# Banded attention: weights times values in float32r passes, with the high and low parts of the values as one stationary operand

## The chip, the cores and the metric

The kernel runs on one core of one Trainium2 chip. The metric is the device time of one execution in microseconds (us), over several executions; lower is better. One execution was also recorded by the profiler, and every row below comes from that one.

## What is computed

Two blocks follow each other on 512 tokens of 1024 features, all in float32. The first block (an mLSTM and stick-breaking attention, then an MLP) is not touched. The second block has two hybrid layers, and each holds a sliding-window attention of 16 heads of 64 features, with two heads for keys and values:

```
s = jnp.einsum('bnqkgd,bnskd->bnkgqs', qb, kw) * ATT_SCALE     # blocks of 128 queries, 256 keys
s = jnp.where(mask, s, NEG_INF)                                # the band: the last 128 keys
p = jax.nn.softmax(jnp.concatenate([s, sink], axis=-1), axis=-1)[..., :-1]
o = jnp.einsum('bnkgqs,bnskd->bnqkgd', p, vw)                  # weights times values: the change is here
...
o_a = o * jax.nn.silu(z_a)
y = jnp.einsum('bse,ed->bsd', jnp.concatenate([o_h, o_a], axis=-1), w_out)
return x + rms_norm_2(y, g_post)
```

The other half of a hybrid layer is a recurrence (`hgrn2`) of 8 heads, whose result `o_h` goes through the first half of `w_out`.

## The kernel before

The large products split each float32 operand into a high and a low part in float32r, a format that TensorE takes in one pass, and add three products (`mm3`, lines 142 to 150: high by high, low by high, high by low). A group is one output tile of 128 by 512, made of 24 such matmuls. `load_w` (lines 127 to 140) brings weights by DMA (queue SP) into three raw buffers `wr`; ScalarE (ACT) makes the high part `wh`, VectorE (DVE) the low part `wl`. Smaller products run as plain float32 matmuls; the profile shows each of those as two records.

**The attention** is `swa_pair(p)`, for two heads each, called eight times a layer. Per head h, in this order:

- scores: 8 float32r matmuls into two banks of PSUM (`xa`, line 531), with stationary operand of 128 columns;
- mask and minimum: four VectorE instructions (line 537) into two pages `prp` of the buffer ring `ha` (4 buffers); four exponentials on ScalarE (line 539), then one small one for the sink (line 543);
- the sum, its reciprocal and four scalings on VectorE (lines 544, 545, 548);
- 7 transposes on TensorE into two banks `xb` (lines 553, 555), copied to `pT` in ring `hb` by ScalarE (lines 557, 559);
- weights times values: 7 float32 matmuls (lines 563, 565) with 64 stationary columns into one bank `po` of tag `xc`. The two heads of a pair share that bank, on 64 partitions each, and one VectorE instruction (line 567) multiplies it by the gate page `zt` and stores `oa[p]`.

**What sets the order.** The code is written in program order with priorities; a scheduler then puts the instructions of each engine into a fixed order, and each engine runs its own list in order. Buffers of one tag are handed out in the order of the code: a tile waits until the one whose buffer it takes is free. In PSUM, tag `xc` has one buffer, and tag `mt` (`K.pmt()`) has one. `mt` is used by the query projection (`proj_qa`, transposes of line 465), and by the loop at line 601 that transposes the eight recurrence heads into `T1`.

The code of a layer runs, as far as it matters here: the last two projections `proj_qa(1)` and `proj_za(1)` (8 groups), pairs 0 to 3 of the attention with a priority above them, the eight transposes into `T1` (line 601, ScalarE line 604, VectorE line 605), pairs 4 to 7, then the output projection `wo1` (8 groups, which need `T1` alone) and `wo2` (8 groups, which need all of `oa`). The results of `wo1` are copied out by ScalarE (line 617); those of the last two blocks of tokens go into pages of tag `on`, which `oa[4]` to `oa[7]` use too.

Of the kernel before, what the change touches and what calls it, by code (L numbers as in the profile page):

```python
# [17 lines left out]
P = 128  # L18
# [40 lines left out]
class Kern:  # L59
# [42 lines left out]
    def above(self, mark):  # L102
        """Priority above everything emitted since mark."""
        return self.tc.high_priority(self.tc.cur_priority - mark + 4000)
# [4 lines left out]
    def rsqrt(self, ms, tag=None, bufs=4):  # L109
        """1/sqrt of a small positive tile."""  # L110
        p, n = ms.shape[0], ms.shape[1]
        y = self.small(n, tag or f"rsy{n}", bufs, p)
        e = self.nhalf[:p, 0:1] if n == 1 else self.nhalf[:p, 0:1].to_broadcast([p, n])
        self.nc.gpsimd.tensor_tensor(y, ms, e, ALU.pow)  # L114
        return y

    def later(self, f):
        """Emit f after the evacuation of the next product."""
        self.new.append(f)
# [5 lines left out]

# [1 line left out]
    def load_w(self, src, n=S, prio=20000):  # L127
# [14 lines left out]
    def mm3(self, ps, st, mv):  # L142
        """ps += sum_k st[k].T @ mv[k], each operand a (hi, lo) pair."""
        nc = self.nc
        n = len(st)
        for k in range(n):
            (sh, sl), (mh, ml) = st[k], mv[k]
            nc.tensor.matmul(ps, sh, mh, start=(k == 0), stop=False)  # L148
            nc.tensor.matmul(ps, sh, ml, start=False, stop=False)  # L149
            nc.tensor.matmul(ps, sl, mh, start=False, stop=(k == n - 1))  # L150
# [24 lines left out]

# [1 line left out]
    def new_T(self):  # L177
# [12 lines left out]
    def bcast2(self, page, src):  # L190
        """A row of 1024 on every partition, as two pages."""
        out = []
        for i in range(2):
            t = page()
            self.nc.sync.dma_start(out=t, in_=src[i * S:(i + 1) * S].partition_broadcast(P))
            out.append(t)
        return out

    def prep(self, gsrc, page, wk, T):
        """Returns f(tb, pages): rms norm of a token block (two [128, 512] pages), transposed and split into T."""  # L200
        nc = self.nc
        g = self.bcast2(page, gsrc)

        def do(tb, x):
            xn = [wk(), wk()]
            ss = [self.small(1, f"ss{i}", 4) for i in range(2)]
            for i in range(2):
                nc.scalar.activation(xn[i], x[i], AF.Square, scale=D ** -0.5, accum_out=ss[i])
            rs = self.rms(ss)
            c = slice(tb * P, (tb + 1) * P)  # L210
            for i in range(2):
                nc.vector.scalar_tensor_tensor(xn[i], x[i], rs, g[i], ALU.mult, ALU.mult)
                ps = self.psum("xa" if i else "xb").rearrange("p (k t) -> p k t", k=4)
                for k in range(4):
                    nc.tensor.transpose(ps[:, k, :], xn[i][:, k * P:(k + 1) * P], self.ident)
                self.split(T[0][i][:, :, c], T[1][i][:, :, c], ps)
        return do

    def rms(self, ss):
        """1/sqrt(ss[0] + ss[1] + eps)."""  # L220
        s = self.small(1, "rmss", 4)
        self.nc.gpsimd.tensor_scalar(s, ss[0], ss[1], EPS, ALU.add, ALU.add)
        return self.rsqrt(s)
# [24 lines left out]
def layer(K, l, xd, win, wout, gpost, lbp, ghead, sinks, out, gnext):  # L248
    """One hybrid layer: K.hT and xd (DRAM rows of x) -> out (DRAM), and the next layer's K.hT."""
    nc, tc = K.nc, K.tc  # L250
    if True:
# [9 lines left out]
        def hb():  # L261
            return page("hb", 4)

        # lower bounds: [128, 8] tiles, feature f = 128 h + p
        lb = K.lc.tile([P, 2, 8], F32, name=f"lb{l}")
# [178 lines left out]
        def rope(dst, ps, tb, nh):  # L444
            """dst, ps: [128, nh * 64]."""
            a = ev()[:, :nh * 64]
# [31 lines left out]
        def proj_kv():  # L478
            quad = K.quad(F32R)
            kT.extend((quad[:, i, :], quad[:, 2 + i, :]) for i in range(2))  # L480
            va.append(page("va", 1).rearrange("p (c d) -> p c d", c=NT))

# [11 lines left out]
            def evac(tb, ps):  # L494
                nc.scalar.copy(va[0][:, tb, :], ps[:, P:2 * P])
                r = ev()
                rope(r[:, 0:P], ps[:, 0:P], tb, 2)
                K.later(lambda: turn(tb, r))
# [13 lines left out]
        def swa_pair(p):  # L512
            kv = p // 4
            zt = page("zs", 2)
            nc.sync.dma_start(out=zt, in_=za_d[p * P:(p + 1) * P, :])
            po = K.psum("xc", 1)
            for e in range(2):
                h = 2 * p + e
                r = slice(64 * e, 64 * e + 64)
                pT = [hb().rearrange("p (s t) -> p s t", s=2) for _ in range(2)]  # L520
                pn, den = K.small(NT, "pn", 4), K.small(NT, "den", 4)
# [27 lines left out]
                for i in range(2):  # L549
                    pt = K.psum("xb").rearrange("p (s t) -> p s t", s=2)  # L550
                    for s in range(2):
                        sb = 2 * i + s
                        nc.tensor.transpose(pt[:, s, 0:P], Ps[sb][0][:, P:2 * P], K.ident)  # L553
                        if sb + 1 < NT:
                            nc.tensor.transpose(pt[:, s, P:2 * P], Ps[sb + 1][0][:, 0:P], K.ident)
                    if i == 0:
                        nc.scalar.copy(pT[i], pt)
                    else:
                        nc.scalar.copy(pT[i].rearrange("p s t -> p (s t)")[:, :384], pt.rearrange("p s t -> p (s t)")[:, :384])
                vv = slice(64 * kv, 64 * kv + 64)  # L560
                for n in range(NT):
                    o = po[r, n * P:(n + 1) * P]
                    nc.tensor.matmul(o, va[0][:, n, vv], pT[n // 2][:, n % 2, 0:P], start=True, stop=(n == 0))  # L563
                    if n:
                        nc.tensor.matmul(o, va[0][:, n - 1, vv], pT[(n - 1) // 2][:, (n - 1) % 2, P:2 * P],  # L565
                                         start=False, stop=True)
            nc.vector.tensor_tensor(oa[p], po, zt, ALU.mult)

# [26 lines left out]

        # head outputs, transposed, head norm gain applied in the split
        T1 = K.new_T()
# [58 lines left out]
def block1(K, xd, prm, win, wout, wup, wdown, bif, gmix, gmlp, out, gnext):  # L656
# [13 lines left out]
    with ExitStack() as octx:  # L670
# [40 lines left out]

# [1 line left out]
        v1 = {}  # L713
# [28 lines left out]

        # gates: rows 0-7 input, rows 32-39 forget; rows 64-103 the products of the low parts of the weights
        raw = ma()[:, :P].rearrange("p (k n) -> p k n", k=KT)
# [173 lines left out]

# [1 line left out]
        qb, ks, kb, vb, rq = {}, {}, {}, {}, {}  # L920

        def proj_qkb(c, is_q):
            """Head norms, then 4 heads transposed: [128 d, 4 heads, 512 t]."""
            quad = bq.tile([P, 4, S], F32, name=K.nm("qk"), tag="q" if is_q else "k", bufs=2)
# [112 lines left out]

# [1 line left out]
    K.stp = K.ctx.enter_context(tc.tile_pool(name="st", bufs=1, reuse_waits="tile"))  # L1039
# [106 lines left out]
```

## Time and profile before

| | |
|---|---|
| median of 3 executions | 1870.59 us (1868.47 to 1870.9) |
| span of the profiled execution | 1868.7 us |
| TensorE (PE) busy | 1828.8 us, 98% |
| VectorE (DVE) busy | 1033.3 us, 55% |
| ScalarE (ACT) busy | 828.5 us, 44% |
| attention heads of layer 1 and of layer 2 | some 1133 to 1305 and 1625 to 1797 us |

The page gives no separate time for the profiled execution; its span lies at the lower end of the timed ones, so that what lies around the span is under about 2 us. PE rows are matmuls and PEld rows the loads of their stationary operand. A matmul's duration is longer than the distance to the next one, since matmuls are pipelined: for a cost, the distance between starts is read. [...]

### The profile page before, as it was taken

The numbers are of one execution on the slowest core, as the hardware profiler recorded it, in microseconds if no ns is written. First come the engines' busy times: TensorE is split into PE (matmuls) and PEld (weight loads), VectorE is DVE, ScalarE is ACT, GpSimd is POOL, SyncE is SP. The second block draws the span as 40 slices with busy tenths as digits, with TensorE's granted clock in tenths as the row PEclk, the third lists the DMA queues.
The fourth block names the chain that finished last, engine by engine and source line by source line (L and its number), as shares of the span: only waits on it lengthen the run. The fifth ranks groups of instructions, "written<-read, shape, count | busy, mean of one in ns | idle before, by whom it ended". The sixth has DMA issues, their size and how long they took to land.

```text
span 1868.7 us, 29367 instructions
## 1 busy us (share of the span) xinstructions
PE 1828.8 (98%) x11696; PEld 1498.3 (80%) x11696; DVE 1033.3 (55%) x2162; ACT 828.5 (44%) x1687; POOL 136.1 (7%) x191
## 2 busy tenths in 40 slices
PE   7999999999999999999999999999999999999998
PEld 5777788787798888888888888878878888888786
DVE  4364545546554444446474666756265648575733
ACT  4456634344342323233443445656344345374641
POOL 1001111010000000000000001100130001101002
PEclk9999999999999999999999999999999999999999
DMA  6252433231432222334323232322343222422222
GB/s 185 60 105 63 102 75 85 67 90 45 147 101 92 90 90 90 106 108 141 111 80 103 69 105 95 108 91 71 105 163 97 92 74 93 127 88 74 74 91 101
DMA packets 103442, 180.09 MB, mean 96 GB/s; under 512 B 8960, under 2 KB 19584, under 8 KB 103304
## 3 DMA queue, kind: packets, MB, share of 16 engines
q1 hardware_dynamic: 103304, 178.20, 31.9%
q8 instruction: 92, 1.51, 0.3%
q14 instruction: 46, 0.38, 0.1%
HBM read 163.48 MB, written 14.70 MB: 95 GB/s over the span
## 4 chain that ended last, share of the span: by engine, by line
PE 89%; DMA 4%; ACT 3%; DVE 2%; issue 1%; POOL 0%; SPq 0%; ACTq 0%; DVEq 0%
PE mm L148 24%; PE mm L150 24%; PE mm L149 24%; DMA wr<-in_w_in_dram 2%; PE xc L563 2%; PE xa L531 1%; PE xc L565 1%; PE xc L993 1%; PE xa L975 1%; PE xb L553 1%; DMA pg<-xs 1%; PE xc L427 1%; ACT wh L136 1%; PE xc L419 1%; PE xa L372 1%
## 5 line engine op out<-in xcount | busy, mean ns | idle before, releaser
L136 ACT CAST wh<-wr 128x1024 fp32r<-128x1024 f32 (+1 forms) x272 | 282.1, 1039 | 327.2 <-PE mm L150 146.6
L137 DVE TENSOR_TENSOR wl<-wr,wh 128x1024 fp32r<-128x1024 f32 (+1 forms) x272 | 328.7, 1214 | 168.6 <-ACT wh L136 80.7
L148 PE MATMUL mm<-wh,hh 128*128 128x512 f32 (+1 forms) x896 | 348.8, 390 | 10.3 <-ACT hh L604 4.4
L149 PE MATMUL mm<-wl,hh 128*128 128x512 f32 (+1 forms) x896 | 348.0, 389 | 0.0
L150 PE MATMUL mm<-wh,hl 128*128 128x512 f32 (+1 forms) x896 | 347.1, 391 | 0.0
L148 PE MATMUL mm<-hh,wh 128*128 128x512 f32 x640 | 255.3, 399 | 6.8 <-ACT pg L730 6.2
L150 PE MATMUL mm<-hh,wl 128*128 128x512 f32 x640 | 253.8, 397 | 0.8 <-DVE wl L137 0.8
L149 PE MATMUL mm<-hl,wh 128*128 128x512 f32 x640 | 253.2, 396 | 0.0
L148 PEld LDWEIGHTS mm<-wh,hh 128*128 128x128 f32 x896 | 169.3, 189 | 45.4 <-ACT hh L604 5.2
L149 PEld LDWEIGHTS mm<-wl,hh 128*128 128x128 f32 x896 | 169.0, 189 | 32.8 <-DVE wl L137 1.1
L150 PEld LDWEIGHTS mm<-wh,hl 128*128 128x128 f32 x896 | 168.1, 189 | 31.6 <-DVE hl L188 0.3
L148 PEld LDWEIGHTS mm<-hh,wh 128*128 128x128 f32 x640 | 121.0, 189 | 34.2 <-ACT pg L730 8.0
L150 PEld LDWEIGHTS mm<-hh,wl 128*128 128x128 f32 x640 | 120.9, 189 | 27.7 <-DVE wl L137 2.0
L149 PEld LDWEIGHTS mm<-hl,wh 128*128 128x128 f32 x640 | 121.0, 189 | 24.8 <-issue 0.2
L148 PE MATMUL mm<-qd,wh 128*128 128x512 f32 (+1 forms) x288 | 105.3, 366 | 0.0
L149 PE MATMUL mm<-qd,wh 128*128 128x512 f32 (+1 forms) x288 | 105.3, 366 | 0.0
L150 PE MATMUL mm<-qd,wl 128*128 128x512 f32 (+1 forms) x288 | 105.1, 366 | 0.0
L148 PE MATMUL mm<-wh,ah 128*128 128x512 f32 x256 | 100.3, 392 | 0.2 <-ACT wk L1075 0.2
L149 PE MATMUL mm<-wl,ah 128*128 128x512 f32 x256 | 99.6, 389 | 0.0
L150 PE MATMUL mm<-wh,al 128*128 128x512 f32 x256 | 99.6, 389 | 0.0
L114 POOL TENSOR_TENSOR sm<-sm,nhalf 128x4 f32<-128x4 f32 (+1 forms) x64 | 59.9, 936 | 505.4 <-DVE sm L436 329.6
L1085 DVE TENSOR_TENSOR qd<-mm,qd 128x512 f32<-128x512 f32 x64 | 44.1, 688 | 58.5 <-PE mm L150 58.4
(294 smaller groups left out, 2768.7 us busy)
## 6 DMA issues: line engine op xcount, KB each, us to landing
wr<-in_w_in_dram SPq DMA_DIRECT2D x160, 512.0 KB, 4.7
wr<-in_w_out_dram SPq DMA_DIRECT2D x40, 512.0 KB, 4.3
wr<-in_w_up_dram SPq DMA_DIRECT2D x32, 512.0 KB, 4.3
wr<-in_w_down_dram SPq DMA_DIRECT2D x32, 512.0 KB, 4.5
zh<-pg SPq DMA_DIRECT2D x16, 256.0 KB, 2.1
pg<-zh SPq DMA_DIRECT2D x16, 256.0 KB, 2.9
za<-pg SPq DMA_DIRECT2D x16, 256.0 KB, 2.0
pg<-za SPq DMA_DIRECT2D x16, 256.0 KB, 2.6
```

What stands on the lines that cost most here:

```text
L114: self.nc.gpsimd.tensor_tensor(y, ms, e, ALU.pow)
L136: nc.scalar.copy(hi, raw)
L137: nc.vector.tensor_tensor(lo, raw, hi.bitcast(F32), ALU.subtract)
L148: nc.tensor.matmul(ps, sh, mh, start=(k == 0), stop=False)
L149: nc.tensor.matmul(ps, sh, ml, start=False, stop=False)
L150: nc.tensor.matmul(ps, sl, mh, start=False, stop=(k == n - 1))
L372: nc.tensor.matmul(pl[32 * j:32 * j + 32, o0 + 32 * c:o0 + 32 * c + 32], k[:, o:o + 32], q[:, o:o + 32])
L419: nc.tensor.matmul(pS[:, c, :], kt[:, c, :], v[c][:, vc])
L427: nc.tensor.matmul(po[:, c, :], ST[:, c, :], v[c][:, vc], start=True, stop=(c == 0))
L531: nc.tensor.matmul(psc[:, i, 2 * P - wi:], qT[p][e][:, t1 - P:t1], kT[kv][j][:, t1 - wi:t1], start=(j == 0), stop=(j == 1))
L563: nc.tensor.matmul(o, va[0][:, n, vv], pT[n // 2][:, n % 2, 0:P], start=True, stop=(n == 0))
L1085: nc.vector.tensor_tensor(t, ps, t, ALU.add)
```

## The change

The values are split into a high and a low part of 64 columns each, side by side, and the weights after the transposes are split into a high and a low part too (`K.split`: ScalarE copies the high part, VectorE subtracts). Per head, 7 float32 matmuls with 64 stationary columns become 8 float32r matmuls with 128 stationary columns, each over up to 256 moving columns: rows 0 to 63 of the bank hold the product with the high part of the values, rows 64 to 127 that with the low part. ScalarE copies the lower half to a page `u`, and VectorE adds the two halves into `oa`. The even head of a pair uses the bank `xc`, the odd one the bank `mt`. `u` comes from the ring `ha`; the low parts of the weights come from a new ring `hq` of 4 buffers. The scratch that is set aside for DMA is set to 4096 bytes a partition. The other edits of the diff take out comments.

```diff
         def proj_kv():
...
-            va.append(page("va", 1).rearrange("p (c d) -> p c d", c=NT))
+            va.append(K.lp.tile([P, 2, NT, P], F32R, name=K.nm("va"), tag="va", bufs=1))
...
             def evac(tb, ps):
-                nc.scalar.copy(va[0][:, tb, :], ps[:, P:2 * P])
+                v3 = ps[:, P:2 * P].rearrange("p (i d) -> p i d", i=2)
+                vh_, vl_ = va[0][:, :, tb, 0:64], va[0][:, :, tb, 64:P]
+                nc.scalar.copy(vh_, v3)
+                nc.vector.tensor_tensor(vl_, v3, vh_.bitcast(F32), ALU.subtract)
...
         def swa_pair(p):
...
-            po = K.psum("xc", 1)
             for e in range(2):
                 h = 2 * p + e
                 r = slice(64 * e, 64 * e + 64)
-                pT = [hb().rearrange("p (s t) -> p s t", s=2) for _ in range(2)]
+                po = K.psum("xc", 1) if e == 0 else K.pmt()
+                pT = [[K.lp.tile([P, S], F32R, name=K.nm("pT"), tag=("hb", "hq")[j], bufs=4) for j in range(2)]
+                      for _ in range(2)]
...
-                    if i == 0:
-                        nc.scalar.copy(pT[i], pt)
-                    else:
-                        nc.scalar.copy(pT[i].rearrange("p s t -> p (s t)")[:, :384], pt.rearrange("p s t -> p (s t)")[:, :384])
-                vv = slice(64 * kv, 64 * kv + 64)
+                    w = slice(0, S if i == 0 else 384)
+                    K.split(pT[i][0][:, w], pT[i][1][:, w], pt.rearrange("p s t -> p (s t)")[:, w])
+
                 for n in range(NT):
-                    o = po[r, n * P:(n + 1) * P]
-                    nc.tensor.matmul(o, va[0][:, n, vv], pT[n // 2][:, n % 2, 0:P], start=True, stop=(n == 0))
-                    if n:
-                        nc.tensor.matmul(o, va[0][:, n - 1, vv], pT[(n - 1) // 2][:, (n - 1) % 2, P:2 * P],
-                                         start=False, stop=True)
-            nc.vector.tensor_tensor(oa[p], po, zt, ALU.mult)
+                    t1 = min((n + 2) * P, S)
+                    for j in range(2):
+                        nc.tensor.matmul(po[:, n * P:t1], va[0][:, kv, n, :],
+                                         pT[n // 2][j][:, n % 2 * 256:n % 2 * 256 + t1 - n * P],
+                                         start=(n == 0 and j == 0), stop=True, skip_group_check=True)
+                u = ha()
+                nc.scalar.copy(u[0:64], po[64:P])
+                nc.vector.tensor_tensor(oa[p][r], po[0:64], u[0:64], ALU.add)
+            nc.vector.tensor_tensor(oa[p], oa[p], zt, ALU.mult)
...
-    nc = bacc.Bacc("TRN2", target_bir_lowering=False, num_devices=1)
+    nc = bacc.Bacc("TRN2", target_bir_lowering=False, num_devices=1, dynamic_dma_scratch_size=4096)
```

The order of the instructions changes with it. On TensorE, in layer 1, near the end of the two last projections, the kernel before has this (L531 are scores of one head, L563 and L565 are weights times values of another, L148 to L150 are matmuls of a projection group):

```order
L553 MATMUL xb_10387<-ident,pg_10368 128x128
L531 MATMUL xa_10467<-qd_8414,qd_8733 128x256 x4
L148 MATMUL mm_9963<-hh_4208,wh_9941 128x512
L149 MATMUL mm_9963<-hl_4210,wh_9941 128x512
L150 MATMUL mm_9963<-hh_4208,wl_9942 128x512
L148 MATMUL mm_9963<-hh_4208,wh_9941 128x512
L149 MATMUL mm_9963<-hl_4210,wh_9941 128x512
L150 MATMUL mm_9963<-hh_4208,wl_9942 128x512
L563 MATMUL xc_10298<-pg_10349,pg_8415 64x128 x2
L565 MATMUL xc_10298<-pg_10349,pg_8415 64x128
```

Projection matmuls stand between the steps of the heads; the longest piece of the list with none between them has 21 matmuls. In the changed kernel, behind the last projection group, it has this (L566 are weights times values of the head in bank `xc_10215`, L535 the scores of the head after the next, L557 and L559 the transposes of the next head):

```order
L566 MATMUL xc_10215<-pT_10217,va_8415 128x256
L566 MATMUL xc_10215<-pT_10218,va_8415 128x256
L566 MATMUL xc_10215<-pT_10219,va_8415 128x256
L566 MATMUL xc_10215<-pT_10218,va_8415 128x128
L566 MATMUL xc_10215<-pT_10219,va_8415 128x128
L535 MATMUL xa_10343<-qd_8414,qd_8736 128x128 x2
L535 MATMUL xa_10343<-qd_8414,qd_8736 128x256 x2
L535 MATMUL xa_10353<-qd_8414,qd_8736 128x256 x4
L557 MATMUL xb_10309<-ident,pg_10286 128x128
L559 MATMUL xb_10309<-ident,pg_10286 128x128
```

Weights times values, scores and transposes follow each other with no matmul of a projection between them; this goes on for 157 matmuls there, and for 100 in a second place, after the first half of `wo1`. Layer 2 has the same two pieces.

On ScalarE, in the first of these pieces, a head's part of the list is this in the changed kernel (L187 copies of the transposed weights, L570 the copy `u` of that head, L543 and L547 the exponentials of the next head):

```order
L187 CAST pT_10337<-xb_10371 128x512
L187 CAST pT_10339<-xb_10378 128x384
L570 COPY pg_10392<-xc_10336 64x512
L543 ACTIVATE pg_10407,sm_10401<-pg_10407,sm_10400 128x128
L543 ACTIVATE pg_10407,sm_10401<-pg_10407,sm_10400 128x256
L543 ACTIVATE pg_10417,sm_10401<-pg_10417,sm_10400 128x256 x2
L547 ACTIVATE sm_10422<-sm_10400,snk_6734 128x4
L187 CAST pT_10396<-xb_10430 128x512
```

The exponentials of a head stand behind the copy `u` of the head ahead of it. In the kernel before, ScalarE's list in the attention has no instruction that reads `xc`, and the steps of two heads are mixed:

```order
L539 ACTIVATE pg_10680,sm_10674<-pg_10680,sm_10673 128x128
L539 ACTIVATE pg_10680,sm_10674<-pg_10680,sm_10673 128x256
L557 COPY pg_10617<-xb_10649 128x512
L539 ACTIVATE pg_10690,sm_10674<-pg_10690,sm_10673 128x256 x2
L543 ACTIVATE sm_10695<-sm_10673,snk_6734 128x4
L559 COPY pg_10618<-xb_10655 128x384
```

The copies of one head's transposed weights stand among the exponentials of another.

## Rows read from the trace of the kernel before

**Rows 1.** The page's first line and TensorE's line: busy us, share, instructions.

```profile
span 1868.7 us, 29367 instructions
PE 1828.8 (98%) x11696; PEld 1498.3 (80%) x11696; DVE 1033.3 (55%) x2162; ACT 828.5 (44%) x1687; POOL 136.1 (7%) x191
```

**Rows 2.** Table by stretch, both attention stretches: start:end, length, busy us by engine, PEclk.

```profile
1130.00:1310.00 180.00, 176.65 (x1042) 146.65 (x1041) 118.17 (x333) 112.34 (x282) 13.89 (x10) 1.00 0.28 90
1630.00:1810.00 180.00, 176.84 (x1037) 146.63 (x1036) 111.35 (x323) 109.25 (x278) 11.22 (x8) 1.00 0.26 84
```

**Rows 3.** Timeline, PE: start us, us of it; weights times values, then scores.

```profile
1226.14 0.65 PE L563 MATMUL xc<-pg,pg 128*64 128x128 f32 x4
...
1227.50 0.38 PE L565 MATMUL xc<-pg,pg 128*64 128x128 f32 x2
...
1253.58 0.63 PE L531 MATMUL xa<-qd,qd 128*128 128x256 f32 x4
1254.05 0.60 PE L601 MATMUL mt<-ident,pg 128*128 128x128 f32 x4
```

**Rows 4.** Line 531, its weight loads: ns min/median/max, first and last start, forms.

```profile
L531 PEld LDWEIGHTS xa<-qd,qd x256: 186/189/247, 1133.7 to 1773.8; 128*128 128x128 f32 x128
```

**Rows 5.** Timeline, PE: two transposes in a row, and a head's last values.

```profile
1255.27 0.27 PE L555 MATMUL xb<-ident,pg 128*128 128x128 f32 x1
1255.38 0.27 PE L553 MATMUL xb<-ident,pg 128*128 128x128 f32 x1
...
1276.16 0.38 PE L565 MATMUL xc<-pg,pg 128*64 128x128 f32 x2
```

**Rows 6.** Timeline, ACT: copies of transposed weights, the sink's exponential, three of another head.

```profile
1255.64 0.59 ACT L557 COPY pg<-xb 128x512 f32<-128x512 f32 x1 [0.26 <-PE xb L555]
1256.12 0.48 ACT L559 COPY pg<-xb 128x384 f32<-128x384 f32 x1
...
1260.04 0.29 ACT L543 ACTIVATE sm<-sm,snk 128x4 f32<-128x4 f32 x1
...
1267.45 0.40 ACT L539 ACTIVATE pg<-pg,sm 128x128 f32<-128x128 f32 x1
...
1267.84 0.50 ACT L539 ACTIVATE pg<-pg,sm 128x256 f32<-128x256 f32 x1
...
1268.33 0.51 ACT L539 ACTIVATE pg<-pg,sm 128x256 f32<-128x256 f32 x1
```

**Rows 7.** Timeline, DVE: sum, reciprocal and scaling of a head; sum of another; line 567.

```profile
1254.39 0.15 DVE L544 TENSOR_TENSOR sm<-sm,sm 128x4 f32<-128x4 f32 x1
1254.58 0.18 DVE L545 RECIPROCAL sm<-sm 128x4 f32<-128x4 f32 x1
1254.80 1.08 DVE L548 TENSOR_SCALAR pg<-pg,sm 128x128 f32<-128x128 f32 x4
...
1260.36 0.16 DVE L544 TENSOR_TENSOR sm<-sm,sm 128x4 f32<-128x4 f32 x1 [2.35 <-ACT sm L543]
...
1276.58 0.69 DVE L567 TENSOR_TENSOR pg<-xc,pg 128x512 f32<-128x512 f32 x1 [2.51 <-PE xc L565]
```

**Rows 8.** Timeline, ACT and DVE: high part, low part; four low parts in a row.

```profile
1289.01 0.63 ACT L187 CAST qd<-pg 128x512 fp32r<-128x512 f32 x1
...
1289.68 0.69 DVE L188 TENSOR_TENSOR qd<-pg,qd 128x512 fp32r<-128x512 f32 x1 [0.23 <-ACT qd L187]
...
1291.76 2.49 DVE L188 TENSOR_TENSOR qd<-pg,qd 128x512 fp32r<-128x512 f32 x4
```

**Rows 9.** Line 537 and the table loads of line 539: ns min/median/max, forms.

```profile
L537 DVE CUSTOM_DVE_ANT_0 pg<-xa,lcst,nsnk x128: 311/478/485, 1142.9 to 1775.8; 128x256 f32<-128x256 f32 x96, 128x128 f32<-128x128 f32 x32
...
L539 ACT ACT_TABLE_LOAD  x10: 1283/1283/1283, 1145.3 to 1738.5; - x10
```

**Rows 10.** Table by stretch, near the end: a full stretch, and the last one.

```profile
1808.00:1812.00 4.00, 4.00 (x19) 3.32 (x18) 0.00 (x0) 0.16 (x1) 0.00 (x0) 1.00 0.00 0
...
1864.00:1868.00 4.00, 0.00 (x0) 0.00 (x0) 1.41 (x2) 0.00 (x0) 0.00 (x0) 0.72 0.37 141
```

## The prediction

> **What bounds the kernel now.** I read the page's engine line first: TensorE is busy for 1828.8 of 1868.7 us [rows 1]. Then the table by stretch, over the two stretches in which the attention heads lie: of 180 us each, TensorE is busy for 176.65 and 176.84, so that 3.3 us of each are idle; VectorE has 118 and 111 us of work there, ScalarE 112 and 109 [rows 2]. So TensorE's list, run end to end, is the time, and a head's long chain over three engines costs nothing, because matmuls of the projections lie between its steps. The reader is to see both in that table: a full TensorE, and two other engines at some 60%, which would not be hidden if they had to wait for each other. The rows that follow are timelines, from which I take distances between starts.
>
> **What it takes off TensorE.** Before, a head's weights times values are 14 records, from 1226.14 to the last pair at 1227.50 plus two steps of 0.11: 1.58 us [rows 3]. After, they are 8 float32r matmuls. The nearest rows are the scores, of the same kind and width: four start 0.47 us before the next instruction, 0.117 each [rows 3]. Six of these and two of 128 columns at 0.11 are 0.92, with the first load some 0.97. That takes 0.61 us off a head, 9.8 off a layer of 16 heads and 19.5 in all. Bounds: 1.1 a head if the eight cost half of what the scores cost; if each had to wait out a load of 0.189 instead of 0.117, 0.58 of the 0.61 is gone. A load of 128 columns lasts 186 to 189 ns [rows 4], which is longer than the 117 ns from one score matmul to the next, so it is hidden there, and I take it as hidden.
>
> [...]
>
> **What it adds elsewhere.** Per head, VectorE gets two subtractions (0.6 us for the one of 512 columns, four of them last 2.49 [rows 8]; 0.55 for the one of 384 as an upper bound) and an addition of 512 columns on 64 partitions, ScalarE a copy of the same shape. Nothing shows 64 partitions; the whole width costs 0.69 and 0.59 [rows 6, 7], I take 0.6 and 0.48 to the next start. That is 1.8 and 0.5 us a head, 28 and 8 a layer, on engines with 60 us to spare in the stretch [rows 2]. By itself it is free. The four small subtractions of `proj_kv` are hidden by its projection, and SP issues the same loads and stores in another order: the loads of gate pages for pairs 4 to 6 now stand ahead of the weights of `wo2`, but these have the second half of `wo1` as cover.
>
> **What it moves: the cover goes.** The bank `mt` is handed out in the order of the code, and the odd heads now use it. Head 1 gets it only after the last transposes of `proj_qa(1)`, head 3 after head 1, the transposes into `T1` after head 7, and `wo1` needs `T1`. So heads 2 to 8 can't run early any more, and nothing that could fill TensorE is ready until they are through. The order shows it: after the last projection group stand 157 matmuls with none of a projection between them, against at most 21 before. This is piece A. Piece B has 100: the last two results of the first half of `wo1` go to pages that `oa[4]` and up take, so the copies stand behind head 14, and heads 11 to 14 run bare.
>
> **The period of a bare head.** In both pieces the engines' lists make a head wait for the one ahead of it: ScalarE's exponentials of head h+1 stand behind the copy `u` of head h, which needs the last weights times values of h. Starting with the copy of the first transposed weights of h, in us:
>
> - cast 0.58 and 0.04 to the subtraction [rows 8], where 1289.01 to 1289.68 is 0.67 with a cast of 0.63: 0.62; the second subtraction 0.60 later, at 1.22, ends by 1.77; the second cast (0.48 after the first [rows 6]) is not late;
> - sixth matmul of weights times values at 1.82, the last at 2.05; it lasts 0.27, and a reader starts 0.04 after the end [rows 5, 7], by the two from 1276.16 on and the reader at 1276.58: `u` at 2.36;
> - exponentials at 2.84, then 0.39 and three times 0.49 [rows 6]: the sink's at 4.70;
> - sum 0.32 after it [rows 6, 7], from 1260.04 to 1260.36: 5.02; reciprocal 0.19 and scalings 0.22 later [rows 7]: 5.43; the third of four, of 1.08 in all, ends at 6.23;
> - fourth transpose at 6.28; the next head's copy starts 0.37 after it [rows 5, 6], from 1255.27 to 1255.64: **6.65**.
>
> VectorE's mask and minimum instructions (0.48 each at most [rows 9]) start at 1.77 and stay ahead of the exponentials; all of VectorE's work is some 5.0 us a head, ScalarE's 3.9. TensorE's work is 0.92 of scores, 7 transposes of 0.11 [rows 5] and 0.92: 2.6 us. A bare head so leaves TensorE idle for 4.0 us.
>
> **Piece A**, from the end of the last projection matmul: some 2.8 us to the copy of head 2 (gate, its product on VectorE, scalings, transposes); 6.65 and a table load of 1.28 [rows 9] to head 3; five times 6.65 to head 8: 44.0. TensorE's work in it: 7 heads of scores 6.4, transposes 5.4, 6 heads of values 5.5: 17.3. Idle 26.7.
>
> **Piece B**, from the copy of head 10: two weight casts stand before `u`, which adds 0.7: 7.35; two periods, 13.3; one with three subtractions of `oa` between sum and scalings, 8.45; then 2.36, `u`, an exponential and a copy of a `wo1` result before the next group has a bank: 3.9. Together 33.0. TensorE's work: 3.4 of transposes, 4.6 of values, 3.7 of scores, 7 projection matmuls of 0.21 (19 in 4 us [rows 10]) 1.5: 13.2. Idle 19.8.
>
> The transposes into `T1` lie between the two with 48 matmuls of `wo1`, as before, and I leave them the 3.3 us of idle that the stretch has now [rows 2]; they could have none or the double. So a layer gains 26.7 and 19.8 of idle time and loses 9.8 of work: 36.7 more. Two layers: 73.4. The span goes from 1868.7 to 1942; what lies around it is under 2 us, and from the median of 1870.6 it gives **1944**.
>
> **The rivals.**
>
> *The clock falls in the bare pieces.* TensorE is busy in them for 39% of the time, in bursts. Its granted clock is 1.00 in both stretches [rows 2], and the one row under that is 0.72, after the last matmul, with TensorE idle throughout [rows 10]; the trace has no stretch that is half busy. [...]
>
> *The heads overlap, and the busiest engine is the bound.* If the lists let a period shrink to VectorE's 5.0 us, twenty periods give back 33: **1911**. Against it speaks the order of ScalarE's list, which has one head in it at a time.
>
> *TensorE stays full* (not slower). One mechanism: the steps of a head find other matmuls or are short enough, and only the 19.5 us come off: **1851**. The point from which it decides is where a bare period costs no more than the change takes off: 36.7 us over ten periods, that is a period of 3.0 instead of 6.65. VectorE's work alone is 5.0, and each engine's list is fixed, so nothing can be pulled between. Records of before with heads and projections interleaved speak for it, and the new order against.
>
> *The loads show*, 0.58 us in the covered heads, some six a layer, since the bare ones don't wait for TensorE: 7 more, **1951**. *The change does nothing of the kind* (the eight matmuls cost as much as the fourteen): 8 us in covered heads, **1952**, inside the range of the first.
>
> **How the numbers follow.** My forecast of 1944 has 0.60, with its own range of 1925 to 1963 (a period of 5.9 to 7.4 gives 15 on either side, the stretch with `T1` 3 a layer). The clock has 0.22, loads or no gain on TensorE 0.07, the overlap 0.06, the full TensorE 0.05. Of the last, 0.04 is faster by over 0.2%, which is about what a measurement of this kernel can tell from no change, and 0.01 within it; slower has the rest. The range leaves out the full TensorE and the ends of the others: 1918 to 1980.
>
> **What would show it.** In the profile of the changed kernel, the table by stretch should show two pieces a layer, of some 44 and 33 us, in which TensorE is busy for about 40% and no engine for more than 80%; TensorE's waits should be led by the lines of the transposes and of weights times values, for VectorE; heads there should start 6.65 us apart; and the eight matmuls of a covered head should start 0.117 apart. The forecast is wrong if TensorE stays at 98%, if heads in the pieces start 5 us apart or less, or if the granted clock falls there.

## The result, and the profile after

The changed kernel takes 1963.56 us (median of 4 executions, 1962.6 to 1964.69), the kernel before 1870.64 beside it: 1.05 times the time, 95% interval 1.0485 to 1.0515. The forecast was 1944, with a range of 1918 to 1980. The sign and the mechanism (heads that run bare) held; the size was short by 19.6 us, and two reasons given on the way were wrong: the bank that was named as the cause, and that the added work on VectorE is free. The experiments show this.

The page of the changed kernel: its first line, the engines (as [rows 1]), and the granted clock in 40 slices of some 49 us.

```profile
span 1962.6 us, 29097 instructions
PE 1865.4 (95%) x11504; PEld 1530.8 (78%) x11504; DVE 1093.8 (56%) x2266; ACT 848.8 (43%) x1719; POOL 133.9 (7%) x191
PEclk9999999999999999999999999588999999995879
```

TensorE has fewer instructions than before and is busy for longer: 1865.4 us instead of 1828.8. The clock line (PEclk, in tenths of full speed) says why. It is 9 throughout, except at one place in each layer, where it reads 5, 8, 8 and 5, 8, 7.

The table by stretch of layer 1 (columns as in [rows 2], PEclk as a share of full speed): with the projections as cover; inside piece A; between the pieces; inside piece B.

```profile
1130.00:1216.00 86.00, 86.00 (x450) 72.40 (x448) 55.73 (x117) 47.73 (x101) 11.62 (x9) 1.00 0.34 108
1224.00:1268.00 44.00, 32.82 (x129) 27.52 (x129) 28.00 (x98) 21.42 (x67) 0.00 (x0) 0.50 0.06 20
1280.00:1304.00 24.00, 22.33 (x115) 17.56 (x114) 14.26 (x30) 12.01 (x25) 0.00 (x0) 1.00 0.08 22
1312.00:1340.00 28.00, 19.40 (x79) 15.63 (x77) 19.17 (x63) 13.84 (x43) 0.00 (x0) 0.56 0.04 14
```

In the pieces the granted clock is 0.50 and 0.56, and TensorE looks busy for 75% and 69% of the time, with work that takes longer at that clock (the ledger below has by how much). No other engine is over 69% there.

One period of a bare head in piece A (timeline; start us, us, engine, line, in brackets the idle time ahead and what ended it):

```profile
1239.38 0.45 PE L557 MATMUL xb<-ident,pg 128*128 128x128 f32 x1 [1.74 <-DVE pg L552]
1239.62 0.42 PE L559 MATMUL xb<-ident,pg 128*128 128x128 f32 x1
1239.84 0.42 PE L557 MATMUL xb<-ident,pg 128*128 128x128 f32 x1
...
1240.51 1.12 ACT L187 CAST pT<-xb 128x512 fp32r<-128x512 f32 x2 [2.00 <-PE xb L559]
...
1241.15 2.48 PE L566 MATMUL xc<-pT,va 128*128 128x256 f32 x8
...
1243.67 0.58 ACT L570 COPY pg<-xc 64x512 f32<-64x512 f32 x1 [2.04 <-PE xc L566]
...
1246.34 0.16 DVE L548 TENSOR_TENSOR sm<-sm,sm 128x4 f32<-128x4 f32 x1 [1.38 <-ACT sm L547]
...
1246.75 1.07 DVE L552 TENSOR_SCALAR pg<-pg,sm 128x128 f32<-128x128 f32 x4
1247.18 0.45 PE L557 MATMUL xb<-ident,pg 128*128 128x128 f32 x1 [1.74 <-DVE pg L552]
...
1248.31 1.12 ACT L187 CAST pT<-xb 128x512 fp32r<-128x512 f32 x2 [2.00 <-PE xb L559]
```

Copy to copy is 7.80 us, and it repeats at 1256.11 and 1263.91. Each engine waits in its turn for another one in the chain, as forecast. Two steps of the chain are longer than forecast, and both are TensorE's. From the copy to `u` it takes 3.16 instead of 2.36. From the first scaling (line 552) to the next copy it takes 1.56 instead of 1.22: transposes now start 0.21 apart instead of 0.11 [rows 5], so the fourth waits for the third and no longer for its scaling. Together that is 1.14 of the 1.15.

A covered head's weights times values (TensorE, timeline), between matmuls of a projection:

```profile
1212.09 1.05 PE L566 MATMUL mt<-pT,va 128*128 128x256 f32 x8
1212.97 0.45 PE L148 MATMUL mm<-hh,wh 128*128 128x512 f32 x1
```

The eight take 0.88 us, against 1.58 for the fourteen of before [rows 3] and a forecast of 0.97.

TensorE's largest waits (by line: us in total, times, longest):

```profile
PE xb L557 <- DVE pg L552: 47.9, 22, 4.1
...
PE xa L535 <- DVE sm L541: 5.9, 2, 3.9
```

**A ledger of layer 1**, worked out by summing the distances between starts of all rows of TensorE's timeline, idle time (gaps of more than 0.15 us) apart, from 1100 us to the first square of the closing norm (1332.10 before, 1375.46 after: 43.4 later): idle time 27.4 more; scores 8.8 and transposes 9.6 more, for the same instructions, since they lie further apart in the pieces (transposes start 0.21 apart instead of 0.11 [rows 5], and a bare head's eight scores some 0.22 instead of 0.117 [rows 3]); weights times values with the other users of their two banks 1.2 more, although the covered heads save 0.7 each; matmuls of projections 3.6 less, because the changed kernel is some 20 of them further on at 1100. So about two fifths of the added time is not idle TensorE but slow TensorE.

### The profile page after: what moved, and what is told of

The parts are those of the page before. It is cut to its first block, busy times and chain, and to the rows that moved or that the text cites. A ratio compares the mean times of both kernels' runs of the same rounds, so it can differ in the third digit from the quotient of the medians.

```text
span 1962.6 us, 29097 instructions
## 1 busy us (share of the span) xinstructions
PE 1865.4 (95%) x11504; PEld 1530.8 (78%) x11504; DVE 1093.8 (56%) x2266; ACT 848.8 (43%) x1719; POOL 133.9 (7%) x191
## 4 chain that ended last, share of the span: by engine, by line
PE 84%; ACT 6%; DVE 4%; DMA 3%; issue 2%; POOL 0%; SPq 0%; DVEq 0%; POOLq 0%; ACTq 0%
PE mm L148 23%; PE mm L149 23%; PE mm L150 23%; ACT pg L543 2%; DMA wr<-in_w_in_dram 2%; PE xc L566 1%; PE mt L566 1%; PE xb L557 1%; PE xc L998 1%; PE xa L980 1%; PE xc L427 1%; DVE wl L137 1%; DVE pT L188 1%; ACT pT L187 1%; ACT wh L136 1%
## 5 line engine op out<-in xcount | busy, mean ns | idle before, releaser
L148 PE MATMUL mm<-wh,hh 128*128 128x512 f32 (+1 forms) x896 | 352.4, 394 | 10.7 <-ACT pg L622 3.3
L150 PE MATMUL mm<-wh,hl 128*128 128x512 f32 (+1 forms) x896 | 348.1, 392 | 0.0
L148 PE MATMUL mm<-hh,wh 128*128 128x512 f32 x640 | 254.0, 397 | 7.1 <-ACT pg L735 6.8
L150 PE MATMUL mm<-hh,wl 128*128 128x512 f32 x640 | 252.9, 395 | 0.8 <-DVE wl L137 0.7
L148 PEld LDWEIGHTS mm<-wh,hh 128*128 128x128 f32 x896 | 170.9, 191 | 48.6 <-ACT hh L609 6.6
L150 PEld LDWEIGHTS mm<-wh,hl 128*128 128x128 f32 x896 | 169.6, 191 | 31.7 <-DVE hl L188 0.5
L148 PEld LDWEIGHTS mm<-hh,wh 128*128 128x128 f32 x640 | 120.6, 188 | 34.2 <-ACT pg L735 8.6
L150 PEld LDWEIGHTS mm<-hh,wl 128*128 128x128 f32 x640 | 120.7, 189 | 27.0 <-DVE wl L137 2.1
L148 PE MATMUL mm<-qd,wh 128*128 128x512 f32 (+1 forms) x288 | 105.3, 366 | 0.0
L150 PE MATMUL mm<-qd,wl 128*128 128x512 f32 (+1 forms) x288 | 105.1, 366 | 0.0
L148 PE MATMUL mm<-wh,ah 128*128 128x512 f32 x256 | 100.4, 392 | 0.0
L150 PE MATMUL mm<-wh,al 128*128 128x512 f32 x256 | 99.7, 389 | 0.0
L557 PE MATMUL xb<-ident,pg 128*128 128x128 f32 x128 | 45.5, 366 | 47.9 <-DVE pg L552 47.9
```

## The experiments

All ratios are to the kernel before, run beside it on the same chip. The last column counts matmuls between two projection matmuls in the attention, a float32 matmul as one; the kernel before has 21.

| what runs | us | ratio, 95% interval | longest bare piece (matmuls) |
|---|---|---|---|
| the changed kernel | 1963.56 | 1.0485 to 1.0515 | 157 |
| bank back (odd heads in `xc`) | 1953.44 | 1.0416 to 1.0457 | 199 |
| page back (`u` in its own buffer) | 1869.29 | 0.9975 to 0.9995 | 113 |
| both back | 1864.89 | 0.9947 to 0.9975 | 30 |
| before, odd heads in `mt` | 1874.0 | 1.0001 to 1.0022 | 70 |
| before, a third page from the ring | 1946.69 | 1.0388 to 1.0417 | 161 |
| before, that page in its own buffer | 1875.8 | 1.0014 to 1.0034 | 26 |
| changed, scores issued three times | 1947.22 | 1.0389 to 1.0423 | 253 |
| changed, `u` copied twice | 1982.5 | 1.0579 to 1.061 | 153 |
| changed, gate and a scaling on GpSimd | 1970.25 | 1.0517 to 1.0554 | 155 |
| both back, gate on GpSimd | 1861.34 | 0.9937 to 0.9962 | 27 |
| both back, gate and one scaling on GpSimd | 1851.06 | 0.987 to 0.9906 | 24 |
| both back, gate and two scalings on GpSimd | 1848.63 | 0.9869 to 0.9902 | 27 |

### What takes the cover away: bank or page

The prediction named the bank `mt`. The other candidate is `u`: each head now takes three pages of `ha`'s four instead of two.

Both back:

```diff
-                po = K.psum("xc", 1) if e == 0 else K.pmt()
+                po = K.psum("xc", 1)
...
-                u = ha()
+                u = K.lp.tile([P, 16, 48], F32, name=K.nm("qx"), tag="qx", bufs=1).rearrange("p n t -> p (n t)")[:, :S]
```

> The changed kernel with both shared resources taken back: odd heads use the bank xc again, not mt, and the page u comes from a buffer of its own (tag qx, free by then), not from the ring ha. The arithmetic of the change stays. In the order, projection matmuls stand between the heads again (longest piece without one: 25 matmuls). If lost cover is the cause of the whole loss: 1851 us (1870.6 less 16 x 2 heads x 0.61), granted clock 1.00 in the attention stretches. If instead the longer chain of a head (three more VectorE steps, one more on ScalarE) costs by itself, it stays above 1871.

1864.89 us, beside 1872.28 for the kernel before. The long bare pieces are gone (the list has 25 matmuls in a row among the covered heads, and 30, not 25, at 1286 to 1296 us, where the last heads end), and the change is worth having, but by some 7 us, not by 19.5; that gap is taken up below.

Only the bank back (the first line of that diff), and only the page back (the second):

> Only the bank taken back (odd heads in xc); u still from the ring ha. If the bank mt alone takes the cover away, as the prediction said: 1851 us. If the ring ha does it too: the order has one piece of 199 matmuls a layer without a projection matmul, some 8.5 heads; at 5.6 us for each bare head ((1963.6 - 1851) / 20) that is 1851 + 17 x 5.6 = 1946.

1953.44. With the bank back, 10 us come off, and some 81 stay (the kernel before has 1872.28 beside it).

> Only the page u taken back (its own buffer); the odd heads still in mt. If the bank alone is the cause, nothing changes: 1964 us. If the ring ha alone is: 1851. If both share it: the order has one piece of 113 matmuls a layer, some 4.7 heads, 1851 + 9.4 x 5.6 = 1904.

1869.29. With the page back, 94 us come off, with the odd heads still in `mt`. This is the cause. The order still has a piece of 113 matmuls without a projection, but the heads overlap in it: first copies of transposed weights (ScalarE, timeline, page back)

```profile
1242.32 1.12 ACT L187 CAST pT<-xb 128x512 fp32r<-128x512 f32 x2 [0.72 <-PE xb L559]
1248.22 1.12 ACT L187 CAST pT<-xb 128x512 fp32r<-128x512 f32 x2 [0.24 <-PE xb L559]
1252.35 0.59 ACT L187 CAST pT<-xb 128x512 fp32r<-128x512 f32 x1 [0.18 <-PE xb L559]
1257.60 0.97 ACT L187 CAST pT<-xb 128x512 fp32r<-128x512 f32 x2 [0.62 <-PE xb L559]
```

start 5.90, 4.13 and 5.25 us apart instead of 7.80 (the ones within the piece 4.1 to 6.7), and TensorE is busy for 20.46 of the 24 us from 1228 to 1252, although the granted clock is 0.72 there (in layer 2's piece, 1720 to 1744, it is 17.82 of 24 at 0.88).

The two suspects, each put alone into the old arithmetic. First the bank: two heads of a pair in `xc` and `mt`, gated half by half.

```diff
-            po = K.psum("xc", 1)
...
+                po = K.psum("xc", 1) if e == 0 else K.pmt()
...
-            nc.vector.tensor_tensor(oa[p], po, zt, ALU.mult)
+                nc.vector.tensor_tensor(oa[p][r], po[r], zt[r], ALU.mult)
```

> The kernel before with one edit: odd heads in the bank mt, even ones in xc, the gate multiplied per half. The arithmetic of before stays (7 float32 matmuls), there is no u and no split. If the bank alone takes the cover of ten heads a layer: 1871 + 20 x 5.0 = some 1970. If it needs the ring ha as well: the order has one piece of 70 matmuls a layer, some 3 heads, 1871 + 6 x 5 = 1900. If the bank does nothing: 1871.

1874.0, 0.1% slower: the bank alone costs almost nothing. Then the page, from the ring, and as a control the same with `u` from its own buffer, as in the run with both back:

```diff
-            nc.vector.tensor_tensor(oa[p], po, zt, ALU.mult)
+                u = ha()
+                nc.scalar.copy(u[r], po[r])
+                nc.vector.tensor_tensor(oa[p][r], u[r], zt[r], ALU.mult)
```

> The arithmetic of the kernel before (float32, 64 stationary columns, the pair in one bank xc), with one thing of the change: each head takes a third page u from the ring ha. ScalarE copies the head's half of the bank to u, VectorE multiplies that by the gate, half by half. Theory (the ring of four pages, not the float32r arithmetic and not the bank mt, takes the cover away): heads run one at a time; the list has a piece of 161 matmuls without a projection, some 5.5 heads a layer; at a period of 7.5 and 3.4 us of TensorE work each, 4.1 idle, 23 a layer: about 1917, up to 1930. Rival (the ring costs nothing by itself, the float32r form is needed): 1871 to 1878.

> The same as the run before it, but u in a buffer of its own instead of the ring; longest piece without a projection 26 matmuls. Theory (the ring): 1871 to 1876, although ScalarE reads the bank and does 0.58 us more a head. Rival (ScalarE's copy behind the last values, or its added work, takes the cover away): as the run with the ring, over 1900.

1946.69 and 1875.8. The same instructions on the same engines, and 71 us lie between the two places of a buffer. The ring takes the cover away by itself; float32r is not needed for it. The forecast of 1917 to 1930 for it was 17 to 30 us short. It had 23 us a layer; the first square of the closing norm comes 31.5 us later than before in layer 1, and layer 2 adds another 44.4. The bare piece is the same list of matmuls in both layers, but the granted clock in it is 0.94 in layer 1 (1277 to 1331) and 0.71 in layer 2 (1803 to 1866), and most of its heads follow each other in 6.7 to 6.9 us there and in 8.2 to 8.6 here.

Why: with two pages a head, four pages hold two heads. With three, the second page of head h+1 is the first of head h, and has to wait until the weights of h are transposed; the first page of h+2 is `u` of h. So two heads can no longer be in flight. That the heads then need more time than the projections last, and so end up bare, is how I read the order; it was not tried by itself.

### Why a bare head took 7.80 and not 6.65

Two theories: the granted clock of 0.50, or a wait that the working had left out. To tell them apart, the scores of most heads that run bare are issued three times, which adds TensorE work (37 us in all) and changes no result:

```diff
-                            for j in range(2):
+                            for j in (0, 1) * (3 if 4 <= h < 10 or h >= 12 else 1):
```

> The changed kernel with more work for TensorE: the score matmuls of heads 4 to 9 and 12 to 15 run three times over (same result), so that TensorE fills most of the gap ahead of the transposes in the bare pieces; the order is otherwise the same. At full clock they fit into the gap (8 more pairs are 1.84 us). If the clock that fell to half in the pieces is what makes a period 7.80 instead of 6.65: granted clock 1.00 there, periods of 6.6 to 6.7, total 1963.6 - 20 x 1.15 - some 5 at the hand-overs = 1936, though TensorE has 37 us more to do. If the clock is not the cause (the chain itself was sized too short): periods of 7.8 and 1964. If the clock falls all the same, the longer scores get onto the chain and a period is 9 or more: 1990 or more.

1947.22, so 16 us less with more work. The table by stretch over the same 32 us of piece A, the changed kernel first, then this one:

```profile
1236.00:1268.00 32.00, 24.32 (x97) 20.40 (x97) 20.64 (x71) 15.64 (x52) 0.00 (x0) 0.50 0.06 17
```

```profile
1236.00:1268.00 32.00, 27.43 (x196) 23.27 (x195) 24.60 (x87) 17.62 (x59) 0.00 (x0) 1.00 0.09 25
```

The clock is 1.00 instead of 0.50, and the heads follow each other in 6.75 us (timeline, ScalarE):

```profile
1247.92 0.97 ACT L187 CAST pT<-xb 128x512 fp32r<-128x512 f32 x2 [1.68 <-PE xb L559]
...
1254.67 0.97 ACT L187 CAST pT<-xb 128x512 fp32r<-128x512 f32 x2 [1.68 <-PE xb L559]
```

Both steps that were long are back near the forecast: 2.43 from the copy to `u` (forecast 2.36) and 1.23 from the first scaling to the next copy (1.22). So the period of 6.65 was right to 0.1 for the clock that it assumed. The total is 11 over the expected 1936: heads whose scores weren't tripled still ran slow (the clock is 0.79 in 1220 to 1236).

Is the chain through `u` the one that sets the period? The copy is made a second time, 0.48 more on ScalarE:

```diff
                 nc.scalar.copy(u[0:64], po[64:P])
+                nc.scalar.copy(u[0:64], po[64:P])
```

> The changed kernel with the copy u made twice (the second stands behind the first exponential of the next head on ScalarE). If the chain through ScalarE sets the period of a bare head: 0.48 more each, 8.28 instead of 7.80, 1963.6 + 20 x 0.48 = 1973. If TensorE or VectorE sets it: 1964.

1982.5. The first copies start 8.28 us apart, as the chain has it to the hundredth (timeline, ScalarE):

```profile
1244.64 1.12 ACT L187 CAST pT<-xb 128x512 fp32r<-128x512 f32 x2 [2.00 <-PE xb L559]
1252.92 1.12 ACT L187 CAST pT<-xb 128x512 fp32r<-128x512 f32 x2 [2.00 <-PE xb L559]
```

The total is 9 over the 1973 that twenty such periods give; where these 9 lie was not settled.

### Where the rest of the gain went once the cover was back

Both back should have given 1851 if only TensorE counted. The table by stretch, 1250 to 1290 us, kernel before, then both back:

```profile
1250.00:1290.00 40.00, 38.12 (x261) 31.55 (x260) 27.75 (x109) 29.54 (x94) 0.00 (x0) 1.00 0.08 25
```

```profile
1250.00:1290.00 40.00, 36.70 (x229) 31.53 (x227) 38.61 (x116) 31.00 (x86) 0.00 (x0) 1.00 0.17 50
```

VectorE (the third of the busy times) went from 27.75 to 38.61 of 40: it is nearly full. TensorE waits for it for 5.3 us between 1130 and 1330 (1.0 before), and for ScalarE for 3.6 (2.3). The gate multiplies two pages in SBUF and is moved to GpSimd, on top of both back, and in a second run one of the four scalings too:

```diff
-            nc.vector.tensor_tensor(oa[p], oa[p], zt, ALU.mult)
+            nc.gpsimd.tensor_tensor(oa[p], oa[p], zt, ALU.mult)
...
-                    nc.vector.tensor_scalar(prw, prw, den[:, n:n + 1], None, ALU.mult)
+                    (nc.gpsimd if n == 3 else nc.vector).tensor_scalar(prw, prw, den[:, n:n + 1], None, ALU.mult)
```

> Both back (odd heads in xc, u in its own buffer) and the product with the gate, both of whose operands lie in SBUF, on GpSimd instead of VectorE: VectorE loses 0.69 us a pair, 5.5 a layer. Theory (with the cover back VectorE is the bound for some 60 us a layer, where the table by stretch has it at 19.45 and 19.15 of 20 us, so that its added 1.8 us a head are not free): about 5 of 8 pairs count, 3.4 a layer, 1864.9 goes to about 1858. Rival (chain latencies, not VectorE): 1864 to 1866.

> As the run with the gate on GpSimd, and the fourth of the four scalings of a head on GpSimd too: VectorE loses another 0.27 us a head, 4.3 a layer. Theory (VectorE is the bound): 3 a layer more in the tight stretch, about 1853. Rival (the scaling now lies on the chain of the head at GpSimd's slower pace, or the chain is the bound anyway): 1858 or more.

1861.34 and 1851.06. The gate alone can't be told from both back (the intervals overlap); with the scaling it is clear, 1.1% under the kernel before. So moving two of VectorE's tasks away gives back some 14 us.

Most of these 14 are not waiting, though. The ledger over the whole span, with the same number of projection matmuls in each profiled execution, has for the kernel before, both back, and gate and one scaling on GpSimd: TensorE's idle time 23.9, 37.0 and 35.7 us; the projection matmuls 1513.5, 1519.6 and 1513.5; a mean granted clock of 0.996, 0.988 and 0.994. With both back the clock is 0.83 in 1230 to 1250 and 0.69 in 1290 to 1300, where the kernel before has 1.00. So with VectorE nearly full TensorE lost in two ways, 13 us of waiting and a clock that falls. Of the 12.6 us between the spans of the last two (1864.6 and 1852.0) only 1.3 are waiting; 6.1 are projection matmuls that run as fast as before again, and most of the rest is the attention's own matmuls. That rests on one execution of each.

A second scaling on GpSimd:

> As the run with the gate and the fourth scaling on GpSimd, and the third scaling there too. Theory (VectorE is the bound while heads are covered): another 0.27 us a head off VectorE, up to 3 a layer, 1851 goes to about 1846. Rival (two scalings of 0.97 us in a row on GpSimd are later than VectorE's four, so that the head's chain gets 0.9 us longer, or the remaining waits are TensorE's for ScalarE): 1851 or more.

1848.63, with an interval that is nearly that of one scaling: no verdict between the two. Both beat the kernel before and the changed one.

The same edit in the changed kernel, where heads are bare:

> The changed kernel (u from the ring, odd heads in mt, a bare piece of 155 matmuls a layer) with the gate and the fourth scaling on GpSimd, the edit that took 14 us off where the heads are covered. Theory (bare heads run at the pace of one head's chain, which neither the gate nor the fourth scaling is on): period stays 7.8, 1960 to 1968. Rival (VectorE's load matters there too): 1945 to 1955.

1970.25, so nothing gained and 6.7 lost; 1960 to 1968 was expected. VectorE's load is worth 14 us with cover and nothing without it. The loss is in the period, 8.09 instead of 7.80; line 552 (its group by line: ns min/median/max) in the changed kernel, then here:

```profile
L552 DVE TENSOR_SCALAR pg<-pg,sm x128: 278/348/351, 1155.3 to 1889.2; 128x256 f32<-128x256 f32 x96, 128x128 f32<-128x128 f32 x32
```

```profile
L552 DVE TENSOR_SCALAR pg<-pg,sm x96: 275/528/578, 1159.7 to 1900.4; 128x256 f32<-128x256 f32 x64, 128x128 f32<-128x128 f32 x32
```

VectorE's scalings last 528 ns beside GpSimd's, and the transposes wait for them: from the first scaling to the next copy it takes 1.80 here (1243.16 to 1244.96) instead of 1.56. The expectation took the fourth scaling to be off the chain; the three that are on it got slower.

## Why the prediction was right or wrong, step by step

- **TensorE sets the time before; the cover goes; the heads run bare in two pieces a layer: right.** TensorE's waits are led by the transposes' line for VectorE (the other line that was named, weights times values, has only 0.7 us), and no engine is near full in the pieces.
- **What it takes off TensorE (0.61 a head): right, and a little small.** 0.88 after against 1.58. The loads of 128 columns stay hidden: eight of 0.19 [rows 4] in a row would be 1.5, more than the 0.88 of the eight matmuls. So the rival in which the loads show, and the one in which the eight save nothing, are out. The trace of before has 186 to 189 ns for a load of 128 columns [rows 4] and 132 to 137 for one of 64 (line 563): each got longer by some 50 ns, and the matmuls still take 0.70 us less.
- **The cause that it named, the bank `mt`: wrong.** The step "So heads 2 to 8 can't run early any more" was read off the code's order of that bank and not held against the other buffer in the diff. The ring of `ha` stands in the same diff and is the cause: 94 us come off with it and 10 with the bank. That the forecast came near all the same is because the pieces were counted in the order itself, which doesn't depend on what made them.
- **The period of a bare head, 6.65: the term that was mis-sized.** It measured 7.80. The chain was right to 0.1 us at full clock (6.75 with the scores tripled), and the clock was the rival that came true; it had a chance of 0.22. By its own signs the main case failed: the granted clock fell in the pieces (to 0.50 and 0.56), and 1963.56 lies just past its range of 1925 to 1963. At 0.50 a bare head took 1.15 us more than forecast: its transposes, 0.21 apart instead of 0.11, become a chain of their own. The weight that I gave to the 1.00 of the full stretches [rows 2] was too much, since they had no bare heads in them. And the working says that the trace has no stretch that is half busy and no other row under 1.00 than the last; it has: 0.51 from 87.40 to 94.30, around the end of a wait of 3.62 us, and the second of these two, behind 4 us in which TensorE was less than half busy (table by stretch, before):

```profile
486.00:490.00 4.00, 1.84 (x9) 1.05 (x8) 1.84 (x3) 1.09 (x3) 0.00 (x0) 1.00 0.36 135
490.00:494.00 4.00, 3.64 (x11) 2.42 (x10) 1.52 (x3) 0.72 (x2) 0.00 (x0) 0.57 0.00 0
```

  In piece A the granted clock is 0.50, and with the scores tripled 1.00 over the same 32 us (1236 to 1268); what sets it, no run here shows.
- **The pieces, 44.0 and 33.0 us: short.** Piece A runs from the last projection's matmul at 1216.90 to the next matmul of `wo1` at 1271.47, some 54 us: six steps from copy to copy give 6.7 of the excess and the start 3.6, since head 2's first copy comes 6.4 us after the last projection and not 2.8. Piece B ends at 1343.60 and is some 7 longer than forecast, 3.3 of them in its first step (10.69 from copy to copy instead of 7.35); nine matmuls behind it run 0.43 apart instead of 0.23 (the granted clock is 0.51 from 1343.60 to 1347.50), 1.8. Together this is 19 a layer, while the whole was short by only 9.8 a layer; 1.6 of the difference is in the next point, the rest was not split up.
- **The idle of the stretch with `T1` left at 3.3: too high.** It is about 1.7 in 1280 to 1304.
- **"By itself it is free" (the work on VectorE): wrong in general, and hidden here by the larger loss.** The working divided 60 us of spare time over the whole stretch of 180 us. The heads lie closer than that: with the cover back, VectorE is busy for 38.61 of 40 us, and some 12 of the 19.5 us are not had; 14 come back when two of its tasks go to GpSimd. The time of the rival at 1851 was reached only that way, and with TensorE at 97% instead of full.
- **The overlap at 5.0 us: not in the changed kernel**, but in the kernel with the page back, whose heads come 4.1 to 6.7 us apart.

## What to carry to other kernels

Count the pages that one iteration takes from each ring and divide: a third page from a ring of four cost 71 us with the old arithmetic and 94 with the new, more than the arithmetic gained. When a diff has two changes that can serialize, look for both before naming one. And ask of the stretch that counts, not of the whole, whether the engine that gets the new work has room: here a cheaper step on TensorE paid in full only after VectorE had been relieved.

## What the runs showed of the hardware

- In the changed kernel's bare heads the granted clock was 0.50, with waits of 1.74 us and TensorE busy for 24.32 of 32 us (1236 to 1268); with the scores of the same heads tripled it was 1.00, with TensorE busy for 27.43.
- The same list of matmuls ran at two clocks. In the kernel before with the third page, the bare piece of layer 1 has a granted clock of 0.96 and that of layer 2 one of 0.70 (table by stretch, 40 us of each), with about the same waits of TensorE for the scalings (18.3 us in seven waits, and 16.9 in seven). Why they differ, no run here shows:

```profile
1280.00:1320.00 40.00, 24.12 (x164) 19.47 (x164) 22.36 (x94) 23.10 (x75) 0.00 (x0) 0.96 0.12 36
```

```profile
1806.00:1846.00 40.00, 28.14 (x136) 23.70 (x137) 19.72 (x82) 19.46 (x61) 0.00 (x0) 0.70 0.13 40
```

- The copy `u` of 64x512 lasts 0.58, a copy of 128x512 0.59 [rows 6]; the addition on 64 partitions (line 571) lasts 0.68, the product with the gate on 128 (line 572) 0.69. In these two pairs half the partitions saved 0.01 us.
- With the gate and one scaling on GpSimd, VectorE's scalings of 128x256 took longer: 523 ns (mean of 64) with bare heads, where the changed kernel has 348 (of 96), and 417 with covered ones, where both back has 345. GpSimd's own scaling, by its spans, which are rough, took 923 with bare heads (median). Whether GpSimd is slowed too, these runs don't show.
